# Six places for split pieces, gathering by two experts, folding by matmul, and fewer native down pieces in a mixture of experts

## The chip, the cores and the metric

The kernel runs on one core of a Trainium2 chip, as one program. Its time is the device time in microseconds (us); 1911.24 us is the median of three runs of the kernel before. TensorE (PE in the rows, its weight loads PEld) multiplies, VectorE (DVE) and ScalarE (ACT) work element by element, GpSimd (POOL) and SyncE (SP) here mostly issue DMA transfers.

## The reference

A small transformer in float32 for 256 tokens of width 1024: a first block (modulated norms, differential attention beside a Fourier mixer, and a hierarchical mixture of experts), and then a second block with four feed-forward layers and two mixers. The change lies in the mixture of experts:

```python
def hier_moe(h, w_rg, b_rg, w_re, b_re, w_gate, w_up, w_down):
    ...
    top_val, top_idx = lax.top_k(e_in, TOP_K)          # 2 of the 8 experts of one group
    gate = p_grp * jax.nn.softmax(top_val, axis=-1)
    expert = grp[:, None] * EXPERTS_PER_GROUP + top_idx
    ...
    def expert_block(args):
        tok, wt, e = args
        xb = h_pad[tok]
        y = (jax.nn.silu(xb @ w_gate[e]) * (xb @ w_up[e])) @ w_down[e]
        return y * wt[:, None]
```

There are 32 experts. `w_gate[e]` and `w_up[e]` are 1024 x 512, `w_down[e]` is 512 x 1024, so that 6.3 MB of weights are read for each expert.

## The kernel before

**Precision.** TensorE has a plain FP32 product and a shorter one of type FP32R. The kernel takes most of its products in FP32R, with each operand split in two: ScalarE casts a weight piece to FP32R (`wh`, line 152), VectorE subtracts the cast from the piece (`wl`, line 153), and TensorE multiplies with both (`split`, line 150). A "native" piece is not split; TensorE multiplies it from its raw buffer in plain FP32.

**The stream of weights.** All weights come in pieces of 128 x 2048 (1 MB), in one list, `stream`. `load` issues the next piece's DMA on SP's queue into one of five `raw` buffers, or during the experts into the one buffer of `rawx`. `run_loads` keeps at most so many loads ahead of the oldest piece that isn't finished. A split piece is finished when its split is emitted (its buffer comes free when VectorE has done `wl`), a native piece when its product is. `ahead(3)` emits splits until three pieces wait, into four pairs of `wh` and `wl` (pool `split`); `take` hands out the next.

**An expert.** Up to 64 tokens of an expert have slots. `hot` makes one-hot matrices `G` for four experts, `gather` multiplies the normed rows (high part `xh` and low part `xl`) with `G` into `XG`, whose 128 columns are the 64 high and the 64 low parts of an expert's tokens. `rows(e, which)` multiplies `XG` as the stationary operand with two pieces of the gate (`which` 0) or up weights (1), 32 matmuls of 512 columns for both, and copies the result to `gu` on ScalarE. Its rows 0 to 63 belong to the high, 64 to 127 to the low parts; `turn` transposes `gu`, sums the two halves, and makes silu(gate) times up, split into `act`. `down` multiplies `act` with the two pieces of the down weights and scales to `yh`, `yl`; `place` transposes `G`, and `scatter` adds `yh` and `yl` to the four banks `bank_acc` with it.

The second down piece of every expert is native (`NATIVE`, all four residues of `e % 4`). The loop over the experts is a pipeline:

```python
for e in range(34):
    if 0 < e < 33: turn(e - 1)
    if e < 32: rows(e, 0); ...; gather(...); rows(e, 1); place(e)
    if e > 1: scatter(e - 2)
    if 0 < e < 33: down(e - 1)
```

The framework puts the emitted instructions in order for each engine; on the chip each engine then takes its own in that fixed order, and a waiting instruction holds what stands behind it.

Of the kernel before, what the change touches and what calls it, by code (L numbers as in the profile page):

```python
# [10 lines left out]
F32 = mybir.dt.float32  # L11
F32R = mybir.dt.float32r
# [6 lines left out]
P = 128  # L19
# [2 lines left out]
EPS = 1e-6  # L22
PIECE = 2048
RAW = 5
NX = 1
NEG = -1e30
SEL = -3e38

# [1 line left out]
class Net:  # L30
    def __init__(self, ctx, tc, I, out):
        self.ctx, self.tc, self.nc, self.I, self.out = ctx, tc, tc.nc, I, out
        self.cp = self.pool(ctx, "const", 1)
        self.rawp = self.pool(ctx, "raw", RAW)
        self.psp = ctx.enter_context(tc.tile_pool(name="psum", bufs=4, space=PSUM))
        self.hp = self.pool(ctx, "resid", 1)
        self.h = [self.hp.tile([P, D], F32, name=f"h{t}") for t in range(T)]
        self.xp = self.pool(ctx, "xT", 1)
        self.sp = self.pool(ctx, "small", 2)
        self.wp = self.pool(ctx, "split", 4)  # L40
        self.stream = []
# [3 lines left out]
        self.extra, self.extended, self.spare, self.slots_raw = {}, set(), 0, RAW  # L45
        self.parts = 1

    def pool(self, ctx, name, bufs):
# [8 lines left out]
    def load(self):  # L57
        src, shape, split = self.stream[self.loaded]
        n = int(np.prod(shape))
        if self.spare and self.loaded < self.moe_end:  # L60
            self.spare -= 1
            self.extended.add(self.loaded)
            raw = self.rawx.tile([P, PIECE], F32, name="rawx")
        else:
            raw = self.rawp.tile([P, PIECE], F32, name="raw")
        dst = self.shaped(raw, shape)
        if len(shape) == 3 and shape[1] == 2 and shape[2] == 256:
            for i in range(2):
                self.nc.sync.dma_start(dst[:, :, i, :], src[:, :, i, :])
        else:  # L70
            self.nc.sync.dma_start(dst, src)
        self.pieces[self.loaded] = raw
        for dst, src in self.extra.get(self.loaded, ()):
            self.nc.sync.dma_start(dst(), src)
        self.loaded += 1
# [7 lines left out]
    def run_loads(self):  # L83
        while self.free in self.done:
            self.done.discard(self.free)
            self.free += 1
        while self.loaded < len(self.stream) and self.loaded < self.free + self.slots_raw:
            self.load()

    def extend(self, ctx, n):  # L90

        self.rawx = ctx.enter_context(self.tc.tile_pool(name="rawx", bufs=n, reuse_waits="tile", side="right"))
        self.spare, self.slots_raw = n, RAW + n
        self.run_loads()

    def finished(self, i):
        self.done.add(i)
        if i in self.extended:
            self.spare += 1
        self.run_loads()  # L100

    def find(self, i, split):
# [4 lines left out]
    def ahead(self, n):  # L107

        while len(self.cutq) < n:
            i = self.find(self.cut, True)  # L110
            if i >= min(self.loaded, self.limit):
                return
            raw, shape = self.pieces[i], self.stream[i][1]
            k = int(np.prod(shape))
            wh = self.wp.tile([P, PIECE], F32R, name="wh")
            wl = self.wp.tile([P, PIECE], F32R, name="wl")
# [715 lines left out]
    def first(self):  # L832
# [3 lines left out]
        with ExitStack() as ctx:  # L836
# [376 lines left out]
            self.extend(self.xctx, NX)  # L1213
# [7 lines left out]
    def route_consts(self):  # L1221
        nc, I, cp = self.nc, self.I, self.cp
        self.idr = cp.tile([P, P], F32R, name="idr")
        nc.vector.tensor_copy(self.idr, self.idf)
        self.slots = cp.tile([P, P], F32, name="slots")
        nc.gpsimd.iota(self.slots, pattern=[[0, 2], [1, 64]], base=0, channel_multiplier=0,
                       allow_small_or_imprecise_dtypes=True)
        self.tri = cp.tile([P, P], F32, name="tri")
        nc.gpsimd.memset(self.tri, 1.0)
        nc.gpsimd.affine_select(out=self.tri, in_=self.tri, pattern=[[1, P]], compare_op=OP.is_gt, fill=0.0,  # L1230
                                base=0, channel_multiplier=-1)
        self.wr = cp.tile([P, 8, 36], F32, name="wr")
        nc.gpsimd.dma_start(self.wr[:, :, :4], I["w_router_group"][0].rearrange("(j p) e -> p j e", j=8))
        nc.gpsimd.dma_start(self.wr[:, :, 4:], I["w_router_expert"][0].rearrange("(j p) e -> p j e", j=8))
# [171 lines left out]
                            nc.vector.tensor_add(self.h[t][:, o], self.h[t][:, o], a)  # L1406


    NATIVE = ((0, 5), (1, 5), (2, 5), (3, 5))

    def native(self, e, n):

# [17 lines left out]
    def moe(self):  # L1430
        nc, I = self.nc, self.I
        self.limit = self.moe_end
        with ExitStack() as ctx:
            mp = self.pool(ctx, "moe", 1)
            XG, G, GT, gu, act, ys, acc = {}, {}, {}, {}, {}, {}, {}

            def hot(g):
# [6 lines left out]
            def gather(g, part):  # L1444

                if part == 0:
                    XG[g] = mp.tile([P, 4, 8, P], F32R, name="XG", bufs=2)
                jp, lo = part // 2, part % 2
                src = self.h2l if lo else self.h2h
                ps = self.bank().rearrange("p (j n) -> p j n", j=2)  # L1450
                for j in range(2):
                    for t in range(T):
                        self.mm(ps[:, j, :], src[t][:, P * (2 * jp + j) : P * (2 * jp + j) + P], G[g][:, t, :, :64],
                                start=t == 0, stop=t == 1)
                copy = nc.vector.tensor_copy if g == 0 and lo else nc.scalar.copy
                dst = XG[g][:, :, 2 * jp : 2 * jp + 2, 64 * lo : 64 * lo + 64].rearrange("p e j s -> p j e s")
                copy(dst, ps.rearrange("p j (e s) -> p j e s", e=4))  # L1457

            def place(e):
                ps = self.bank().bitcast(F32R)  # L1460
# [18 lines left out]
                return self.take_raw() if self.native(e, n) else self.take()  # L1479

            def rows(e, which):
                x = XG[e // 4][:, e % 4]
                ps = self.bank()
                for q in range(2):
                    product(ps, x, None, piece(e, 2 * which + q), 4, 4 * q, 7)
                    self.ahead(3)
                sb = mp.tile([P, 512], F32, name=f"gu{which}", bufs=1)

                nc.scalar.copy(sb.rearrange("s (a p) -> s a p", a=4), ps.rearrange("s (p a) -> s a p", a=4))
                gu[e, which] = sb  # L1490

            def turn(e):
                z = []
                for which in range(2):
# [9 lines left out]
                self.split(A[:, :, :64], A[:, :, 64:], z[0])  # L1504
                act[e] = A

            def down(e):
# [27 lines left out]
            self.second_rows(gnr)  # L1535
            self.parts = 4
            hot(0)
            for part in range(8):
                gather(0, part)
            self.weights(mp)  # L1540
            for e in range(34):
                if e == 1:
                    self.parts = 1
                if 0 < e < 33:
                    turn(e - 1)
                if e < 32:
                    rows(e, 0)
                    if e % 4 == 0 and e < 28:
                        hot(e // 4 + 1)
                if e < 32:  # L1550
                    if e < 28:
                        for i in range(2):
                            gather(e // 4 + 1, 2 * (e % 4) + i)
                    rows(e, 1)
                    place(e)
                if e > 1:
                    scatter(e - 2)
                if 0 < e < 33:
                    down(e - 1)
# [105 lines left out]
```

## Time and profile before

| | before |
|---|---|
| median of 3 runs | 1911.24 us (1909.47 to 1917.49) |
| the profiled execution | 1913.98 us, its span 1912.2 us |
| busy in the span: PE, DVE, ACT | 1837.8, 1327.7, 1146.4 us |
| mean granted TensorE clock | 0.99 of full |
| read from memory | 447.9 MB, 235 GB/s over the span |

The profile is of one execution. An engine's busy time is the time in which it has an instruction under way; matmuls overlap, so the step from start to start tells what one costs in a row of them, and a mean duration tells how long one takes to run through. A wait row names who waited and for whom. "Idle" in brackets is what the engine stood just before an instruction.

### The profile page before, as it was taken

How to read it: one execution, taken by the hardware profiler on the slowest of the kernel's cores; microseconds unless marked ns; L12 is line 12 of the kernel's file. 1: busy time of each engine (PE TensorE's matmuls, PEld its weight loads, DVE VectorE, ACT ScalarE, POOL GpSimd, SP SyncE). 2: the span in 40 equal slices, each digit the busy share in tenths (PEclk: the TensorE clock that was granted, in tenths of full speed). 3: DMA queues.
4: the chain of work that ended last, by engine and by line, in shares of the span. 5: the costliest groups of instructions: out<-in, count | busy, mean ns of one | idle time of the engine just before them, and what ended most of it. 6: DMA issues, size and time to landing. Idle time of an engine off the chain costs nothing.

```text
span 1912.2 us, 23030 instructions
## 1 busy us (share of the span) xinstructions
PE 1837.8 (96%) x8352; PEld 1439.9 (75%) x8352; DVE 1327.7 (69%) x2116; ACT 1146.4 (60%) x1924; POOL 41.8 (2%) x74
## 2 busy tenths in 40 slices
PE   6899699999999999999999999999999999999998
PEld 3677577766667666678888888887888888887886
DVE  2887788888888888865558765556555776765554
ACT  3555587778777777754456654446444755555443
POOL 2000000000000000000000000000000010100000
PEclk9999899999999999999999999999999999999999
DMA  9784398999999999865555455554555556665551
GB/s 301 257 284 144 111 340 356 349 357 353 351 357 352 353 365 367 277 220 177 179 179 178 155 176 198 198 186 153 190 198 198 182 172 198 199 218 191 181 180 43
DMA packets 189495, 450.51 MB, mean 236 GB/s; under 512 B 10170, under 2 KB 119066, under 8 KB 164802
## 3 DMA queue, kind: packets, MB, share of 16 engines
q1 hardware_dynamic: 185284, 437.26, 64.5%
q0 software_dynamic: 3808, 11.25, 2.1%
q8 instruction: 66, 1.08, 0.2%
q10 hardware_dynamic: 288, 0.52, 0.1%
q14 instruction: 49, 0.40, 0.1%
HBM read 447.92 MB, written 1.07 MB: 235 GB/s over the span
## 4 chain that ended last, share of the span: by engine, by line
PE 71%; DVE 8%; ACT 5%; issue 3%; DMA 1%; DVEq 0%; ACTq 0%; SPq 0%
PE bank_w L144 50%; PE bank_acc L144 17%; DVE wl L153 6%; ACT wh L152 3%; DMA raw<-w_up 1%; PE bank_w L1497 1%; PE bank_w L299 1%; ACT XG L1457 0%; PE bank_w L230 0%; ACT xh L233 0%; PE bank_w L702 0%; ACT L175 0%; DVE G L1440 0%; DVE yl L1521 0%; PE bank_w L490 0%
## 5 line engine op out<-in xcount | busy, mean ns | idle before, releaser
L153 DVE TENSOR_TENSOR wl<-raw,wh 128x512 fp32r<-128x512 f32 (+3 forms) x977 | 862.9, 936 | 301.4 <-ACT wh L152 299.0
L152 ACT CAST wh<-raw 128x512 fp32r<-128x512 f32 (+3 forms) x977 | 746.0, 823 | 285.2 <-PE bank_w L144 207.2
L144 PE MATMUL bank_w<-wh,xh 128*128 128x512 f32 (+2 forms) x1056 | 406.4, 385 | 4.1 <-ACT xh L233 3.4
L144 PE MATMUL bank_w<-wh,xl 128*128 128x512 f32 (+2 forms) x1056 | 402.7, 382 | 1.0 <-DVE xl L234 1.0
L144 PE MATMUL bank_w<-wl,xh 128*128 128x512 f32 (+2 forms) x1056 | 402.1, 381 | 0.0
L144 PEld LDWEIGHTS bank_w<-wh,xh 128*128 128x128 f32 x1056 | 199.0, 188 | 42.5 <-ACT xh L233 6.3
L144 PEld LDWEIGHTS bank_w<-wh,xl 128*128 128x128 f32 x1056 | 198.9, 188 | 38.0 <-DVE xl L234 2.5
L144 PEld LDWEIGHTS bank_w<-wl,xh 128*128 128x128 f32 x1056 | 199.0, 188 | 35.0 <-issue 0.2
L144 PE MATMUL bank_w<-wl,XG 128*128 128x512 f32 x512 | 208.7, 408 | 13.6 <-DVE wl L153 11.2
L144 PE MATMUL bank_w<-wh,XG 128*128 128x512 f32 x512 | 211.0, 412 | 0.1
L144 PE MATMUL bank_acc<-wh,th 128*128 128x512 f32 x352 | 144.2, 410 | 0.0
L144 PEld LDWEIGHTS bank_w<-wl,XG 128*128 128x128 f32 x512 | 96.0, 188 | 56.4 <-DVE wl L153 37.6
L144 PE MATMUL bank_acc<-wh,tl 128*128 128x512 f32 x352 | 137.7, 391 | 0.0
L144 PE MATMUL bank_acc<-wl,th 128*128 128x512 f32 x352 | 137.6, 391 | 0.0
L292 ACT ACTIVATE silu<-bank_w,rs 128x256 f32<-128x256 f32 x88 | 41.9, 476 | 155.4 <-PE bank_w L144 155.4
L294 DVE SCALAR_TENSOR_TENSOR hid<-bank_w,rs,silu 128x256 f32<-128x256 f32 x88 | 42.6, 484 | 116.7 <-ACT silu L292 113.3
L144 PEld LDWEIGHTS bank_w<-wh,XG 128*128 128x128 f32 x512 | 96.4, 188 | 23.2 <-issue 5.3
L144 PE MATMUL bank_w<-rawx,act 128*128 128x512 f32 x240 | 107.8, 592 | 0.0
L144 PEld LDWEIGHTS bank_w<-rawx,act 128*128 128x128 f32 x240 | 45.4, 189 | 45.5 <-issue 43.1
L144 PEld LDWEIGHTS bank_acc<-wh,tl 128*128 128x128 f32 x352 | 66.1, 188 | 14.1
L144 PEld LDWEIGHTS bank_acc<-wl,th 128*128 128x128 f32 x352 | 66.4, 189 | 11.2
L144 PEld LDWEIGHTS bank_acc<-wh,th 128*128 128x128 f32 x352 | 66.2, 188 | 11.1
(407 smaller groups left out, 2195.3 us busy)
## 6 DMA issues: line engine op xcount, KB each, us to landing
raw<-ffn_w_in SPq DMA_DIRECT2D x176, 512.0 KB, 4.7
raw<-w_up SPq DMA_DIRECT2D x64, 1024.0 KB, 7.9
raw<-w_gate SPq DMA_DIRECT2D x62, 1024.0 KB, 7.5
raw<-ffn_w_out SPq DMA_DIRECT2D x44, 1024.0 KB, 5.7
raw<-w_down SPq DMA_DIRECT2D x34, 1024.0 KB, 7.8
rawx<-w_down SPq DMA_DIRECT2D x30, 1024.0 KB, 6.4
raw<-w_ada SPq DMA_DIRECT2D x24, 1024.0 KB, 6.5
raw<-a_w_in SPq DMA_DIRECT2D x12, 1024.0 KB, 4.9
```

The costliest lines, as they stand in the source:

```text
L144: self.nc.tensor.matmul(*a, **k)
L152: self.nc.scalar.copy(h, src)
L153: self.nc.vector.tensor_sub(l, src, h.bitcast(F32))
L292: nc.scalar.activation(s, ps[:, :256], AF.Silu, scale=self.rs[t])
L294: nc.vector.scalar_tensor_tensor(hid[c, t], ps[:, 256:], self.rs[t], s, op0=OP.mult, op1=OP.mult)
L299: nc.tensor.transpose(ps[:, r, :], hid[c, t][:, P * r : P * r + P], self.idf)
L1497: nc.tensor.transpose(ps[:, P * a : P * a + P], gu[e, which][:, P * a : P * a + P], self.idf)
```

## The change

Four edits, in the mixture of experts:

- The buffer `rawx` goes. A pool `splitx` with two more pairs, `whx` and `wlx`, comes for the time of the experts; of every six splits two go there. `ahead(3)` stays.
- `XG` holds two experts rather than four (two buffers, as before). A gather matmul has 128 columns rather than 256, there are 32 of them for two experts rather than for four, and a copy out of PSUM still has 512 columns.
- `turn` multiplies `gu` with a constant `fold` (two identities of 64 x 64 above each other), which transposes and sums in one; eight transposes, two sums on VectorE and their two tiles go.
- The second down piece is native in the odd experts only.

The space for the descriptors of GpSimd's DMAs is set to 4096 bytes of a partition.

```diff
-            raw = self.rawx.tile([P, PIECE], F32, name="rawx")
-        else:
-            raw = self.rawp.tile([P, PIECE], F32, name="raw")
+        raw = self.rawp.tile([P, PIECE], F32, name="raw")
...
-        while self.loaded < len(self.stream) and self.loaded < self.free + self.slots_raw:
+        while self.loaded < len(self.stream) and self.loaded < self.free + RAW:
             self.load()
...
+            pool, x = self.wp, ""
+            if self.wx and i < self.moe_end:
+                self.cuts += 1
+                if self.cuts % (4 + SX) < SX:
+                    pool, x = self.wx, "x"
+            wh = pool.tile([P, PIECE], F32R, name="wh" + x)
+            wl = pool.tile([P, PIECE], F32R, name="wl" + x)
...
+        self.fold = cp.tile([P, 64], F32, name="fold")
+        nc.vector.tensor_add(self.fold, self.idf[:, :64], self.idf[:, 64:])
...
-    NATIVE = ((0, 5), (1, 5), (2, 5), (3, 5))
+    NATIVE = ((1, 5), (3, 5))
...
-                ps = self.bank().rearrange("p (j n) -> p j n", j=2)
-                for j in range(2):
+                e0 = 2 * (g % 2)
+                ps = self.bank().rearrange("p (j n) -> p j n", j=4)
+                for j in range(4):
                     for t in range(T):
-                        self.mm(ps[:, j, :], src[t][:, P * (2 * jp + j) : P * (2 * jp + j) + P], G[g][:, t, :, :64],
-                                start=t == 0, stop=t == 1)
+                        self.mm(ps[:, j, :], src[t][:, P * (4 * jq + j) : P * (4 * jq + j) + P],
+                                G[g // 2][:, t, e0 : e0 + 2, :64], start=t == 0, stop=t == 1)
...
             def turn(e):
-                z = []
+
+                ps = self.bank().rearrange("p (w a s) -> p w a s", w=2, a=4)
                 for which in range(2):
-                    ps = self.bank()
                     for a in range(4):
-                        nc.tensor.transpose(ps[:, P * a : P * a + P], gu[e, which][:, P * a : P * a + P], self.idf)
-                    r = mp.tile([P, 4, 64], F32, name=f"sum{which}", bufs=1)
-                    nc.vector.tensor_reduce(r, ps.rearrange("p (a i s) -> p a s i", a=4, i=2), axis=AX.X, op=OP.add)
-                    z.append(r)
-                nc.scalar.activation(z[0], z[0], AF.Silu)
-                nc.vector.tensor_mul(z[0], z[0], z[1])
+                        self.mm(ps[:, which, a, :], gu[e, which][:, P * a : P * a + P], self.fold, start=True, stop=True)
+                z = mp.tile([P, 4, 64], F32, name="z", bufs=1)
+                nc.scalar.activation(z, ps[:, 0], AF.Silu)
+                nc.vector.tensor_mul(z, z, ps[:, 1])
...
-            for part in range(8):
+            for part in range(4):
                 gather(0, part)
...
-                    if e < 28:
+                    if e < 30:
                         for i in range(2):
-                            gather(e // 4 + 1, 2 * (e % 4) + i)
+                            gather(e // 2 + 1, 2 * (e % 2) + i)
...
-    nc = bacc.Bacc("TRN2", target_bir_lowering=False, num_devices=1)
+    nc = bacc.Bacc("TRN2", target_bir_lowering=False, num_devices=1, dynamic_dma_scratch_size=4096)
```

The edits also move instructions in the fixed orders. ScalarE's order before, from the up copy of expert 26 to the gate copy of expert 27 (`sum` is the silu, `act` the copy of its split, `wh` the casts of pieces):

```order
L1489 COPY gu_5549<-bank_w 128x512
L1501 ACTIVATE sum_5603<-sum_5603 128x256
L152 CAST act<-sum_5603 128x4x64
L152 CAST wh<-raw 128x2048
L1520 ACTIVATE yh<-bank_w,gslot 128x512 x2
L152 CAST wh<-raw 128x2048
L1457 CAST XG<-bank_w 128x2x4x64
L152 CAST wh<-raw 128x2048
L1457 CAST XG<-bank_w 128x2x4x64
L152 CAST wh<-raw 128x2048
L1489 COPY gu_5646<-bank_w 128x512
```

The same place of ScalarE's order after, between the same two copies (`z` is the silu; the down piece that ends ahead of `yh` is a native one, that of expert 25):

```order
L1488 COPY gu_5764<-bank_w 128x512
L1464 COPY GT<-bank_w 128x256
L148 CAST wh<-raw 128x2048
L1517 ACTIVATE yh<-bank_w,gslot 128x512 x2
L148 CAST wh<-raw 128x2048
L1498 ACTIVATE z<-bank_w 128x256
L148 CAST whx<-raw 128x2048
L1456 CAST XG<-bank_w 128x4x2x64
L148 CAST act<-z 128x4x64
L148 CAST whx<-raw 128x2048
L1488 COPY gu_5857<-bank_w 128x512
```

The first cast now stands ahead of the silu, and the silu and the copy of `act` have moved behind the second `yh`; four casts stand between the two copies in both orders.

Earlier in the stage the order after is another. ScalarE from the up copy of expert 10 to the first XG copy behind the gate copy of expert 11:

```order
L1488 COPY gu_3440<-bank_w 128x512
L148 CAST wh<-raw 128x2048
L1464 COPY GT<-bank_w 128x256
L148 CAST wh<-raw 128x2048
L1517 ACTIVATE yh<-bank_w,gslot 128x512 x2
L148 CAST wh<-raw 128x2048
L1498 ACTIVATE z<-bank_w 128x256
L148 CAST act<-z 128x4x64
L148 CAST wh<-raw 128x2048
L1488 COPY gu_3533<-bank_w 128x512
L1456 CAST XG<-bank_w 128x4x2x64
```

The first cast behind the up copy is here that of the next expert's first up piece; at expert 26 it is that of the next expert's first gate piece. Two pieces more are cast ahead of the up copy here.

On TensorE, at the down piece and the turn of expert 26, before:

```order
L144 MATMUL bank_w<-wh,act 128x512 x2
L1497 MATMUL bank_w<-idf,gu_5510 128x128 x4
L1497 MATMUL bank_w<-idf,gu_5549 128x128 x4
L144 MATMUL bank_w<-wl,act 128x512
L144 MATMUL bank_w<-wh,act 128x512
L144 MATMUL bank_w<-wl,act 128x512 x2
L144 MATMUL bank_w<-wh,act 128x512
L144 MATMUL bank_w<-wl,act 128x512
L144 MATMUL bank_w<-rawx,act 128x512 x4
L144 MATMUL bank_w<-wh,XG 128x512
```

And after:

```order
L140 MATMUL bank_w<-wh,act 128x512 x2
L140 MATMUL bank_w<-fold,gu_5716 128x64 x4
L140 MATMUL bank_w<-fold,gu_5764 128x64
L140 MATMUL bank_w<-wl,act 128x512
L140 MATMUL bank_w<-wh,act 128x512
L140 MATMUL bank_w<-wl,act 128x512 x2
L140 MATMUL bank_w<-wh,act 128x512
L140 MATMUL bank_w<-wl,act 128x512
L140 MATMUL bank_w<-raw,act 128x512 x4
L140 MATMUL bank_w<-fold,gu_5764 128x64 x3
```

Five of the eight products with `fold` stand ahead of the native piece and three behind it; before, all eight transposes stood ahead of it.

## Rows read from the trace of the kernel before

**Rows 1.** Busy by stretch: start:end, length, PE, PEld, DVE, ACT, POOL, clock, DMA, GB/s.

```profile
262.00:770.00 508.00, 494.09 (x2121) 354.55 (x2119) 431.31 (x331) 382.30 (x399) 0.59 (x1) 1.00 0.94 358
830.00:1912.20 1082.20, 1069.26 (x5005) 890.54 (x5003) 662.75 (x1348) 581.73 (x1217) 19.95 (x35) 1.00 0.54 179
```

**Rows 2.** The tile rawx: ns min/median/max, first and last start in us.

```profile
L71 SPq DMA_DIRECT2D rawx<-w_down x30: 327/328/328, 258.3 to 769.7; - x30
```

**Rows 3.** TensorE in time over one expert: start, length in us.

```profile
396.91 0.64 PE L144 MATMUL bank_w<-G,xh 128*128 128x256 f32 x4
...
397.39 1.09 PE L144 MATMUL bank_acc<-yh,GT 128*128 128x512 f32 x4
...
398.32 0.39 PE L144 MATMUL bank_w<-wl,XG 128*128 128x512 f32 x1
...
398.55 0.39 PE L144 MATMUL bank_w<-wh,XG 128*128 128x512 f32 x1
...
403.70 0.28 PE L1462 MATMUL bank_w<-idr,G 128*128 128x128 f32 x2
...
408.55 1.03 PE L1497 MATMUL bank_w<-idf,gu 128*128 128x128 f32 x8
...
410.80 3.59 PE L144 MATMUL bank_w<-rawx,act 128*128 128x512 f32 x8
```

**Rows 4.** Who waited for whom, 262 to 770 us: total, times, longest.

```profile
ACT gu L1489 <- PE bank_w L144: 52.3, 31, 3.0
...
PEld bank_w L144 <- DVE wl L153: 36.2, 69, 1.9
ACT sum L1501 <- DVE sum L1499: 29.5, 27, 2.4
```

**Rows 5.** Groups by shape, 262 to 770 us: busy us, mean ns, idle before.

```profile
L153 DVE TENSOR_TENSOR wl<-raw,wh 128x2048 fp32r<-128x2048 f32 x143 | 326.6, 2291 | 51.7 <-ACT wh L152 49.8
L152 ACT CAST wh<-raw 128x2048 fp32r<-128x2048 f32 x142 | 271.6, 1917 | 3.4 <-DMA raw<-w_gate 1.7 <-PE bank_w L144 1.4 <-DMA raw<-w_up 0.2
...
L144 PE MATMUL bank_w<-rawx,act 128*128 128x512 f32 x232 | 104.2, 592 | 0.0
...
L1499 DVE TENSOR_REDUCE sum<-bank_w 128x256 f32<-128x512 f32 x60 | 38.9, 686 | 10.4 <-PE bank_w L1497 10.4
...
L1457 ACT CAST XG<-bank_w 128x512 fp32r<-128x512 f32 x52 | 30.5, 592 | 0.4 <-PE bank_w L144 0.4
L1497 PE MATMUL bank_w<-idf,gu 128*128 128x128 f32 x232 | 30.1, 272 | 0.0
```

**Rows 6.** ScalarE in time from one up copy on.

```profile
408.28 0.59 ACT L1489 COPY gu<-bank_w 128x512 f32<-128x512 f32 x1 [1.75 <-PE bank_w L144]
...
409.91 0.42 ACT L1501 ACTIVATE sum<-sum 128x256 f32<-128x256 f32 x1 [1.04 <-DVE sum L1499]
...
411.03 0.40 ACT L152 CAST act<-sum 128x256 fp32r<-128x256 f32 x1 [0.71 <-DVE sum L1502]
...
411.34 1.89 ACT L152 CAST wh<-raw 128x2048 fp32r<-128x2048 f32 x1
...
414.43 0.69 ACT L1520 ACTIVATE yh<-bank_w,gslot 128x512 fp32r<-128x512 f32 x1 [0.60 <-PE bank_w L144]
```

**Rows 7.** Plain FP32 products of few columns: router's loads in time; attention's group.

```profile
206.66 0.97 PEld L144 LDWEIGHTS bank_w<-wr,xaT 128*128 128x128 f32 x8 [0.91 <-ACT xaT L1250]
...
L144 PE MATMUL bank_acc<-v,aT 128*128 128x128 f32 x64 | 8.4, 276 | 0.0
```

**Rows 8.** The chain that ended last, at the stage's start.

```profile
226.82 1.85 PE bank_w L144 x7
...
233.62 4.97 PE bank_w L144 x24
```

**Rows 9.** DMA issues: count, KB each, median us to landing.

```profile
raw<-w_gate SPq DMA_DIRECT2D x62, 1024.0 KB, 7.5
...
grp<-b_ln_b POOLq DMA_DIRECT2D x8, 192.0 KB, 6.3
```

More of the change, by code (lines that the diff above doesn't have):

```diff
@@ L24 @@
 RAW = 5
-NX = 1
+SX = 2
 NEG = -1e30
@@ L44, in __init__ @@
         self.pieces = {}
-        self.extra, self.extended, self.spare, self.slots_raw = {}, set(), 0, RAW
+        self.extra, self.wx, self.cuts = {}, None, 0
         self.parts = 1
@@ L59, in load @@
         n = int(np.prod(shape))
-        if self.spare and self.loaded < self.moe_end:
-            self.spare -= 1
-            self.extended.add(self.loaded)
-            raw = self.rawx.tile([P, PIECE], F32, name="rawx")
-        else:
-            raw = self.rawp.tile([P, PIECE], F32, name="raw")
+        raw = self.rawp.tile([P, PIECE], F32, name="raw")
         dst = self.shaped(raw, shape)
@@ L86, in run_loads, with extend @@
             self.free += 1
-        while self.loaded < len(self.stream) and self.loaded < self.free + self.slots_raw:
+        while self.loaded < len(self.stream) and self.loaded < self.free + RAW:
             self.load()
[L90 to L94, printed above, removed]
+    def extend(self, pool):
+        self.wx, self.cuts = pool, 0
     def finished(self, i):
         self.done.add(i)
-        if i in self.extended:
-            self.spare += 1
         self.run_loads()
@@ L114, in ahead @@
             k = int(np.prod(shape))
-            wh = self.wp.tile([P, PIECE], F32R, name="wh")
-            wl = self.wp.tile([P, PIECE], F32R, name="wl")
+            pool, x = self.wp, ""
[5 more added lines that the diff above has]
+            wl = pool.tile([P, PIECE], F32R, name="wl" + x)
             for o in range(0, k, k // self.parts):
@@ L1212, in first @@
             c2.close()
-            self.extend(self.xctx, NX)
             self.route_pre(1, ap, a2)
@@ L1434, in moe @@
             mp = self.pool(ctx, "moe", 1)
+            self.extend(self.pool(ctx, "splitx", SX))
             XG, G, GT, gu, act, ys, acc = {}, {}, {}, {}, {}, {}, {}
@@ L1446, in gather @@
                 if part == 0:
-                    XG[g] = mp.tile([P, 4, 8, P], F32R, name="XG", bufs=2)
-                jp, lo = part // 2, part % 2
+                    XG[g] = mp.tile([P, 2, 8, P], F32R, name="XG", bufs=2)
+                jq, lo = part // 2, part % 2
                 src = self.h2l if lo else self.h2h
-                ps = self.bank().rearrange("p (j n) -> p j n", j=2)
-                for j in range(2):
+                e0 = 2 * (g % 2)
+                ps = self.bank().rearrange("p (j n) -> p j n", j=4)
+                for j in range(4):
                     for t in range(T):
-                        self.mm(ps[:, j, :], src[t][:, P * (2 * jp + j) : P * (2 * jp + j) + P], G[g][:, t, :, :64],
-                                start=t == 0, stop=t == 1)
+                        self.mm(ps[:, j, :], src[t][:, P * (4 * jq + j) : P * (4 * jq + j) + P],
+                                G[g // 2][:, t, e0 : e0 + 2, :64], start=t == 0, stop=t == 1)
                 copy = nc.vector.tensor_copy if g == 0 and lo else nc.scalar.copy
-                dst = XG[g][:, :, 2 * jp : 2 * jp + 2, 64 * lo : 64 * lo + 64].rearrange("p e j s -> p j e s")
-                copy(dst, ps.rearrange("p j (e s) -> p j e s", e=4))
+                dst = XG[g][:, :, 4 * jq : 4 * jq + 4, 64 * lo : 64 * lo + 64].rearrange("p e j s -> p j e s")
+                copy(dst, ps.rearrange("p j (e s) -> p j e s", e=2))
             def place(e):
@@ L1481, in rows @@
             def rows(e, which):
-                x = XG[e // 4][:, e % 4]
+                x = XG[e // 2][:, e % 2]
                 ps = self.bank()
@@ L1492, in turn @@
             def turn(e):
-                z = []
+                ps = self.bank().rearrange("p (w a s) -> p w a s", w=2, a=4)
                 for which in range(2):
-                    ps = self.bank()
                     for a in range(4):
-                        nc.tensor.transpose(ps[:, P * a : P * a + P], gu[e, which][:, P * a : P * a + P], self.idf)
-                    r = mp.tile([P, 4, 64], F32, name=f"sum{which}", bufs=1)
-                    nc.vector.tensor_reduce(r, ps.rearrange("p (a i s) -> p a s i", a=4, i=2), axis=AX.X, op=OP.add)
-                    z.append(r)
-                nc.scalar.activation(z[0], z[0], AF.Silu)
-                nc.vector.tensor_mul(z[0], z[0], z[1])
+                        self.mm(ps[:, which, a, :], gu[e, which][:, P * a : P * a + P], self.fold, start=True, stop=True)
+                z = mp.tile([P, 4, 64], F32, name="z", bufs=1)
+                nc.scalar.activation(z, ps[:, 0], AF.Silu)
+                nc.vector.tensor_mul(z, z, ps[:, 1])
                 A = mp.tile([P, 4, P], F32R, name="act", bufs=2)
-                self.split(A[:, :, :64], A[:, :, 64:], z[0])
+                self.split(A[:, :, :64], A[:, :, 64:], z)
                 act[e] = A
```

## The prediction

> **What bounds the kernel now.** I read the busy time by stretch first. The mixture of experts fills 226 to 790 us, and its even part, 262 to 770 us, is where all four edits act. There TensorE is busy 494 of 508 us, VectorE 431, ScalarE 382, and the DMA engines are 0.94 busy at 358 GB/s; the 1082 us from 830 us on are TensorE at 99% with the DMA at 0.54, and no edit touches that code [rows 1]. So two resources are near full in the stage at once, and the reader should look for the slack of each.
>
> The period comes from the loads of the native down pieces, one an expert: 30 of them from 258.3 to 769.7 us, 511.4 / 29 = **17.63 us an expert** [rows 2].
>
> Busy TensorE counts the running out of each matmul, so I rebuilt its work from starts. A 512-column FP32R matmul follows the last one after 0.23 (398.32 to 398.55; four from 397.39 to 398.32 take 0.93), a 256-column gather matmul after 0.12 (four from 396.91 to 397.39) [rows 3]. Eight transposes take 1.03 with the last one's 0.27, so 0.109 each; eight native instructions 3.59 with the last one's 0.59, so 0.428 each [rows 3, 5]. A piece of 4 native products shows 8 records: a plain FP32 product is two instructions. An expert's work: rows 32 x 0.23 = 7.36, split down piece 8 x 0.23 = 1.84, native piece 8 x 0.428 = 3.42, scatter 8 x 0.23 = 1.84, gather 8 x 0.12 x 28/32 = 0.84, turn 8 x 0.109 = 0.87, place 0.28: **16.45**. The other 1.2 us of the period is TensorE standing.
>
> Why it stands: mostly for the second half of a split, wl from VectorE (36.2 us in the table of waits), while ScalarE itself loses 52.3 us at the gu copies and 29.5 at the sums [rows 4]. One expert shows the loop. The up copy starts at 408.28; the silu waits 1.04 for VectorE's sums, and the next cast starts only at 411.34, 3.06 later; the second yh starts at 414.43, when the native piece is done, and ends 6.84 after the copy [rows 6]. Three casts and two XG copies follow in ScalarE's order (3 x 1.92 + 2 x 0.59 = 6.94, less about 0.1 for each of five overlaps: 13.3), then wl (2.29) and the last eight matmuls (1.84): 17.4 [rows 5]. That is the period. Before is thus a **chain through ScalarE, VectorE and TensorE**, with one cast of reserve at each up copy.
>
> **The change part by part.**
> *Native pieces in every second expert.* 16 pieces go from 3.42 to 1.84: -1.58 x 16 = **-25.3 us** of TensorE. ScalarE and VectorE each split 16 pieces more (1.92 and 2.29 us): half of that an expert, +0.96 and +1.15 [rows 5].
> *Turn by matmul.* 8 one-record transposes become 8 plain FP32 products, 16 instructions, each with its own 128-column weights. No such product with 64 columns stands in the even part. The nearest row has 36 columns: eight loads back to back take 0.97 with 0.19 for the last, 0.111 each, however few columns follow [rows 7]. So 16 x 0.111 = 1.78 against 0.87: +0.91 x 32 = **+29 us** of TensorE. It frees VectorE of two sums of 0.686 an expert [rows 5], and takes a station out of the silu's chain.
> *Gather by two experts.* 256 matmuls of 256 columns become 512 of 128. FP32R products of 128 columns are not in the trace. Lower bound: the FP32R transposes in place, the second 0.06 after the first (0.28 less the 0.22 that one takes) [rows 3]; upper bound: a plain FP32 product of 128 columns, two records of 8.4 / 64 = 0.131, so 0.26 [rows 7]. I take 0.111, since weights of the same size must be loaded for each and the 36-column row shows that this alone sets the step. In the loop 480 x 0.111 = 53.3 against 224 x 0.12 = 26.9: **+26 us**. The copies stay two an expert.
> The Trainium skill, "TensorE: Matmul & The Clock Gate", section "Back-to-back issue gap", gives about 81 ns for a matmul of 128 columns and 131 ns for one of 512 in a stream of loads and matmuls. This trace's 512-column step is 0.23, so I do not follow it; by it the gather would cost 480 x 0.03, an estimated 14 us less.
> *Six places for split pieces.* They take nothing off any engine; they let casts run further ahead. The raw buffers fall from six to five, so that all places together go from ten to eleven. In ScalarE's printed order I counted casts against the pieces used up by each up copy: before, one cast of reserve from expert 5 on; after, two to six up to expert 17, and one or two from 18 on.
> *Start.* The first gather fills one XG of two experts: four copies rather than eight. Its matmuls run from 226.82 to 233.6, waiting on copies, and the first rows start at 233.62 [rows 8]. With half of the copies I take **-2.5 us** (0 to -3.4, half of it).
> *The smaller descriptor space and the fold constant* I cost at nothing: the POOL queue's loads are for the stages behind, where 1082 us of TensorE work cover them; without that cover one such load is 6.3 us late [rows 1, 9].
>
> TensorE after, per expert: 7.36 + 1.84 + 0.28 + (3 x 1.84 + 3.42) / 2 + 16 x 0.111 x 30/32 + 1.78 = **17.4**, 0.95 more than before and 0.23 under the present period. The change trades TensorE's standing for TensorE's work. ScalarE's busy 382 / 28.8 = 13.3 rises to 14.3, VectorE's 15.0 falls by 0.2 [rows 1]. The DMA needs 0.94 x 17.63 = 16.6 us an expert, still under 17.4.
>
> **The sum.** Experts 2 to 17 have reserve, so that the chain above is cut and TensorE paces them: 17.4 and about 0.1 for what is left of waits, -0.13 x 18 = -2.3 (with the first two).
> From 18 on the printed order again has one cast of reserve, and I follow the chain. With a native piece: the rest of the scatter 0.46, split down piece 1.84, five turn products 1.11, native 3.42, and 0.2 until ScalarE sees it: the second yh ends at 7.7 rather than 6.84. Then cast, silu, cast, XG, act, cast: 3 x 1.92 + 0.42 + 0.59 + 0.40 - 0.5 = 6.7, wl 2.29, eight matmuls 1.84: 18.5. Without one: copy and cast of the second down piece end at 2.45, its wl at 4.74, its matmuls at 6.1, the second yh at 7.0; three casts, XG and act 6.75 - 0.4, wl, matmuls: 17.5. Mean 18.0, +0.37 for about 12 experts: +4.5 [rows 5, 6].
> -2.3 + 4.5 - 2.5 = -0.3 us: **no change**. The profiled execution took 1913.98 (span 1912.2 and 1.8 around it), 2.7 above the median of 1911.24; taken from there the sum gives 1913.7, from the median 1911. I say 1912. This kernel's measurement tells about 0.5%, 9.6 us, from no change.
>
> **The rivals.**
> A, slower: the supply binds in all experts. A native piece now holds one of only five raw buffers until TensorE has used it, and loads are issued in stream order, so the fifth load behind it cannot be issued before. Five pieces of 17.63 / 6 us are the whole cover of a landing of 7.5 and a split of 4.2 [rows 9, 5]. For it: the DMA has 0.94 x 17.63 = 16.6 of 17.4 to do. Against: three pieces behind the native one are already split by then. It decides once a hole of more than 1.6 us (twice 17.4 - 16.6) opens per native piece. Then each expert takes 18.0 to 18.4: +11 to +23 us less the start, 1920 to 1932.
> B, slower: a 128-column FP32R product costs like plain FP32: 480 x 0.15 = +72, 1984. Only the bound of rows 7 speaks for it.
> C, faster: the loads of FP32R weights step at 0.06 as in place: 480 x 0.05 = 24 us less TensorE; the DMA's 16.6 becomes the bound at 16.8, so about 20 less: 1892. The 36-column row speaks against it, though it is plain FP32. The skill's 81 ns, as cited, would be part of this.
> D, no change or just faster: the late order does not bind, because the earlier reserve is never used up on the chip. TensorE paces all 30: -0.23 x 30 - 2.5 = -9.4, 1902.
>
> **How the numbers follow.** Forecast 0.55 (1903 to 1921), A 0.20, B 0.04, C 0.06, D 0.15. Faster by over 0.5% is under 1901.7: C, a good third of D and a little of the forecast's lower end, 0.13. Slower is over 1920.8: B, most of A and the forecast's upper end, 0.30. The rest, 0.57, is no change. 1900 to 1930 leaves out C, B, and the ends of A and D: two in ten.
>
> **What would show it.** In the changed kernel's even part: fold matmuls in steps of 0.11, 128-column gather matmuls in steps of 0.11 (0.06 is C, 0.22 and more is B); loads of a second-expert native piece 35 us apart in the first half and 36 in the second; the waits of TensorE for wl near nothing up to expert 17 and back after it; ScalarE's sum waits gone. If the native loads are 36 or more apart from the start, with the DMA share under 0.9 and ScalarE waiting for raw, it is A. The prediction is wrong above all if the reserve counted in the printed order is not what paces the chip, or if the small matmuls are not held by their weight loads.

## The result, and the profile after

The changed kernel took **1925.24 us** (median of 5 runs, 1924.58 to 1928.19), the kernel before 1911.33 on the same chip: a ratio of 1.0071, 95% interval [1.0052, 1.009]. It is slower by 0.7%, and beyond the 1920.8 from which the prediction called it slower. The profiled execution of after took 1927.08 us with a span of 1925.3, 13.1 more than the span of before.

First the busy time of the kernel after by stretch, with the columns of [rows 1]: the even part of the experts, the stages behind it, and two stretches of 100 us inside the even part.

```profile
262.00:770.00 508.00, 500.75 (x2552) 403.73 (x2550) 412.44 (x282) 403.64 (x409) 0.58 (x1) 1.00 0.93 347
830.00:1925.30 1095.30, 1082.44 (x5048) 900.55 (x5046) 665.86 (x1354) 582.18 (x1219) 19.96 (x35) 1.00 0.54 179
...
300.00:400.00 100.00, 100.00 (x519) 81.58 (x518) 82.44 (x55) 82.41 (x84) 0.00 (x0) 1.00 0.93 352
600.00:700.00 100.00, 96.82 (x490) 77.41 (x490) 79.20 (x52) 78.58 (x80) 0.00 (x0) 1.00 0.93 340
```

TensorE never stands in the first stretch of 100 us and does 519 matmuls there; in the second it stands 3% and does 490. VectorE, ScalarE and the loads slow down with it, from 352 to 340 GB/s. So the stage has two regimes. Where one ends shows in the place step, two transposes an expert: its rows in both kernels, each over three stretches. The last numbers are its first and last start, so eight, ten and thirteen experts lie between them. Before:

```profile
L1462 PE MATMUL bank_w<-idr,G x18: 220/224/227, 243.0 to 368.5; 128*128 128x128 f32 x18
L1462 PE MATMUL bank_w<-idr,G x22: 221/223/227, 368.5 to 546.5; 128*128 128x128 f32 x22
L1462 PE MATMUL bank_w<-idr,G x28: 220/223/230, 546.4 to 776.5; 128*128 128x128 f32 x28
```

And after:

```profile
L1461 PE MATMUL bank_w<-idr,G x18: 221/224/229, 244.0 to 374.8; 128*128 128x128 f32 x18
L1461 PE MATMUL bank_w<-idr,G x22: 221/225/229, 374.8 to 549.0; 128*128 128x128 f32 x22
L1461 PE MATMUL bank_w<-idr,G x28: 220/224/232, 549.0 to 786.2; 128*128 128x128 f32 x28
```

The 13.1 us fall apart like this (in rounded parts, 13.0). The first place is 1.0 later. Experts 0 to 8 take 130.8 instead of 125.5: +5.3. Experts 8 to 18 take 174.2 instead of 178.0, **17.42 an expert** instead of 17.80: -3.8. Experts 18 to 31 take 237.2 instead of 230.1, 18.25 instead of 17.70: +7.1. From the last place to the end it is 1139.1 instead of 1135.7: +3.4. The kernel after wins only in the middle. The 18.25 is a mean: from its 25th place to its 29th (657.5 and 732.4 us) an expert takes 18.7.

The steps of the small matmuls stand in TensorE's timeline of after (start, length):

```profile
404.15 1.00 PE L140 MATMUL bank_w<-G,xh 128*128 128x128 f32 x8
404.99 1.06 PE L140 MATMUL bank_w<-G,xl 128*128 128x128 f32 x8
405.89 0.45 PE L140 MATMUL bank_w<-wh,XG 128*128 128x512 f32 x1
...
413.48 3.59 PE L140 MATMUL bank_w<-raw,act 128*128 128x512 f32 x8
416.91 1.89 PE L140 MATMUL bank_w<-fold,gu 128*128 128x64 f32 x16
418.61 0.48 PE L140 MATMUL bank_w<-whx,XG 128*128 128x512 f32 x1
```

Sixteen gather matmuls of 128 columns take 405.89 - 404.15 = 1.74, so 0.109 each; sixteen turn instructions of 64 columns (eight products) take 1.70, 0.106 each; eight native ones 3.43, 0.429 each, as in [rows 3].

The waits of after that answer to [rows 4], 262 to 770 us (total, times, longest):

```profile
DVE wl L149 <- ACT wh L148: 53.5, 54, 2.4
ACT yh L1517 <- PE bank_w L140: 41.4, 37, 2.6
ACT gu L1488 <- PE bank_w L140: 38.1, 28, 3.0
...
PEld bank_w L140 <- DVE wl L149: 8.1, 11, 1.6
...
ACT wh L148 <- DMA raw<-w_down: 2.4, 3, 1.3
```

The waits of TensorE's weight loads for wl fall from 36.2 to 8.1 (2.2 more are for `wlx`), and all of these lie behind 550 us; the sum waits of ScalarE are gone. The casts wait little for loads from memory (2.4 for down pieces, 3.1 in all). In the late stretch the chain that ended last (start, length, what) reads:

```profile
634.55 4.86 PE bank_w L140 x24
...
647.35 0.02 issue
647.37 1.38 ACT yh L1517 x2
648.75 1.80 ACT whx L148
650.56 0.02 issue
650.58 2.30 DVE wlx L149
652.88 0.04 issue
652.93 4.74 PE bank_w L140 x23
```

The path leaves TensorE for the two scaled outputs (`yh`), then one cast and one subtraction, 5.5 us in all, and comes back to it with the next piece. So the cast that TensorE needs next stands in ScalarE's order just behind a copy that waits for TensorE.

### The profile page after: what moved, and what is told of

Same layout as the page of the kernel before. It is cut to its first block, busy times and chain, and to the rows that moved or that the text cites. A ratio compares the mean times of both kernels' runs of the same rounds, so it can differ in the third digit from the quotient of the medians.

```text
span 1925.3 us, 24032 instructions
## 1 busy us (share of the span) xinstructions
PE 1857.9 (96%) x8864; PEld 1501.4 (78%) x8864; DVE 1316.4 (68%) x2067; ACT 1176.7 (61%) x1942; POOL 41.8 (2%) x74
## 4 chain that ended last, share of the span: by engine, by line
PE 80%; DVE 3%; ACT 3%; issue 1%; ACTq 0%; DVEq 0%
PE bank_w L140 59%; PE bank_acc L140 19%; DVE wl L149 2%; ACT wh L148 1%; PE bank_w L295 1%; DVE wlx L149 1%; ACT whx L148 0%; ACT yh L1517 0%; PE bank_w L226 0%; ACT xh L229 0%; PE bank_w L698 0%; DVE xl L230 0%; ACT L171 0%; PE bank_w L1461 0%; PE bank_w L486 0%
## 5 line engine op out<-in xcount | busy, mean ns | idle before, releaser
L149 DVE TENSOR_TENSOR wl<-raw,wh 128x512 fp32r<-128x512 f32 (+3 forms) x930 | 768.4, 881 | 304.6 <-ACT wh L148 303.4
L148 ACT CAST wh<-raw 128x512 fp32r<-128x512 f32 (+3 forms) x930 | 666.3, 778 | 289.1 <-PE bank_w L140 207.5
L149 DVE TENSOR_TENSOR wlx<-raw,whx 128x2048 fp32r<-128x2048 f32 (+1 forms) x68 | 135.8, 2006 | 30.2 <-ACT whx L148 30.1
L140 PE MATMUL bank_w<-wl,XG 128*128 128x512 f32 x340 | 134.8, 396 | 5.4 <-DVE wl L149 5.2
L140 PE MATMUL bank_w<-wh,XG 128*128 128x512 f32 x340 | 136.4, 401 | 0.0
L148 ACT CAST whx<-raw 128x2048 fp32r<-128x2048 f32 (+1 forms) x68 | 113.4, 1683 | 5.2 <-PE bank_w L140 4.2
L140 PEld LDWEIGHTS bank_w<-wl,XG 128*128 128x128 f32 x340 | 63.9, 188 | 21.1 <-DVE wl L149 8.4
L140 PE MATMUL bank_acc<-wh,xh 128*128 128x512 f32 x160 | 67.7, 423 | 6.3 <-ACT xh L148 5.3
```

The lines of the kernel that those rows point to most:

```text
L140: self.nc.tensor.matmul(*a, **k)
L148: self.nc.scalar.copy(h, src)
L149: self.nc.vector.tensor_sub(l, src, h.bitcast(F32))
```

## The experiments

Each ratio is to the kernel before, measured beside it on the same chip. "In reserve" are pieces whose cast stands ahead of a copy in ScalarE's order and whose rows that copy does not need.

**Theory R, first form: the casts in reserve at each gu copy set the pace.** Four kernels. The first and the second put each gu copy of the kernel after, and of before, behind the last cast asked for:

```diff
-                nc.scalar.copy(sb.rearrange(...), ps.rearrange(...))
+                with self.tc.issue_after(self.lastcast.ins):
+                    nc.scalar.copy(sb.rearrange(...), ps.rearrange(...))
```

> The kernel after, with one thing changed: each gu copy is put behind the last cast emitted ahead of it in ScalarE's order, so that at least three pieces are cast beyond the rows it waits for; no work is added or taken away. Theory R (the reserve in ScalarE's order paces the late experts): from expert 18 on the pair falls from about 37.4 to 34.8 us, 11 us less, about 1914. Rival S (supply: five raw buffers and the DMA pace them): the casts then wait for raw and the time stays at 1925 or grows.

Measured: 1925.13 us, ratio 1.005 [1.0031, 1.0069], as slow as after. That is S's number, but not its reason: the casts wait 2.1 us for loads between 262 and 770 us. The printed order kept three casts in reserve at the up copies to the end, but the slow experts stayed (233.5 us from 18 to 31, after 237.2). ScalarE's waits of this run, 600 to 770 us, say where the wait went:

```profile
ACT yh L1519 <- PE bank_w L141: 19.2, 13, 2.6
ACT GT L1465 <- PE bank_acc L141: 11.8, 9, 2.4
```

In after the same stretch has 17.6 for yh, 14.3 for gu and 1.6 for GT. The gu waits are gone; yh waits a little more, and GT (the copy of the transposed `G`) has taken their place. The expectation looked at one of three kinds of copy that wait for TensorE.

> The kernel before with the same one change of order. Theory R: the experts from 6 on fall from 17.5 (18.8 with a new G) to TensorE's 16.45 or the DMA's 16.6, 25 to 30 us less, about 1883. Rival S: the DMA and six raw buffers already pace them, no change, 1911.

Measured: 1933.78 us, 1.0097 [1.0079, 1.0116], slower than either theory said. In the kernel before the turn follows the up copy closely, and TensorE now waits for gu at the transposes (600 to 770 us):

```profile
PEld bank_w L1499 <- ACT gu L1491: 10.3, 9, 1.3
```

**The kernel after with the turn of before** (eight transposes and two sums instead of eight fold products of two instructions each):

```diff
-                        self.mm(ps[:, which, a, :], gu[e, which][:, P * a : P * a + P], self.fold, start=True, stop=True)
+                        nc.tensor.transpose(ps[:, P * a : P * a + P], gu[e, which][:, P * a : P * a + P], self.idf)
+                    nc.vector.tensor_reduce(r, ps.rearrange("p (a i s) -> p a s i", a=4, i=2), axis=AX.X, op=OP.add)
```

> The kernel after with the turn of before (eight transposes, two sums on VectorE). Theory R with TensorE's work as counted: 0.9 us less an expert, and the printed order keeps five to six casts of reserve to the end; 16.5 an expert, about 1895 (1900 if VectorE's 16.7 binds). Rival: VectorE or the supply binds and the matmul turn was worth its price: 1925 or more.

Measured: 1922.98 us, 1.0044 [1.0032, 1.0056]: a miss, although the printed reserve stayed at five or six. TensorE has less to do, but waits for VectorE's second half of the outputs (`yl`), and ScalarE for the sums (300 to 770 us):

```profile
ACT sum L1498 <- DVE sum L1496: 50.8, 26, 3.5
...
PEld bank_w L140 <- DVE yl L1518: 35.4, 25, 1.8
PE bank_w L140 <- DVE yl L1518: 24.4, 23, 1.3
```

The casts also wait 21.9 us for loads in this stretch, far more than in after; which of these waits sets this run's pace stays open. So a reserve of casts alone does not make TensorE the pace, and the turn by matmul by itself did not make the change slow.

**The kernel after with four places** (SX = 0):

> The kernel after with four places for split pieces rather than six. Theory R: the reserve in the printed order falls to one or two at expert 12 rather than 18, six experts more run at 18.7 rather than 17.4: 8 us more, about 1933. Rival: the places bind nowhere, 1925.

Measured: 1937.62 us, 1.0118 [1.01, 1.0137]. The first eight experts are as in after, but the slow experts begin in the next ten (180.5 us instead of 174.2):

```profile
L1460 PE MATMUL bank_w<-idr,G x18: 221/224/229, 244.0 to 374.5; 128*128 128x128 f32 x18
L1460 PE MATMUL bank_w<-idr,G x22: 221/225/229, 374.5 to 555.0; 128*128 128x128 f32 x22
```

Here R was right in the place, and some 5 us low in the time: the stock sets where the slow stretch begins. What sets its pace was still open; the loads (the prediction's rival A) were the next suspect.

**Theory L: the loads.** More load buffers, by the mechanism that the kernel before had (NX extra ones; the second run has SX = 0 and NX = 2):

```diff
-SX = 2
+SX = 1
+NX = 1
...
+            self.extend_raw(self.xctx, NX)
```

> The kernel after with one extra load buffer from the start of the experts (six in all, as before the change) and five places for split pieces instead of six. Theory L (the loads are the supply: with five load buffers they bring 340 GB/s in the slow stretch, so the 12.6 MB of a pair of experts take 37 us): at the 357 GB/s that six buffers brought in the kernel before, a pair takes 35.2 us or less, the seven slow pairs lose some 13 us, and the time is 1912 (1905 to 1918). Theory R (the stock of split pieces, worn down by the place of the casts in ScalarE's order, is what ends): one place fewer begins the slow stretch earlier, as with four places, and the time is 1931 (1925 to 1938).

Measured: 1925.81 us, 1.0065 [1.0045, 1.0084]. L missed. It lies at the edge of R's range, but R's reason failed: with one place fewer the slow stretch did not begin earlier (experts 0 to 18 in 305.1 us, after 305.0).

> The kernel after with two extra load buffers (seven in all) and four places for split pieces. It differs from the run with four places and five load buffers (1937.6) in the load buffers alone. Theory L: the loads come at 360 GB/s or more, TensorE's 34.8 us a pair is reached nearly everywhere, and the time is 1912 (1904 to 1920). Theory R: as with four places before, 1937 (1931 to 1943).

Measured: 1924.91 us, 1.0054 [1.0033, 1.0074]. Neither number. The place rows of this run:

```profile
L1476 PE MATMUL bank_w<-idr,G x38: 221/225/229, 247.0 to 551.7; 128*128 128x128 f32 x38
L1476 PE MATMUL bank_w<-idr,G x28: 220/224/230, 551.7 to 788.3; 128*128 128x128 f32 x28
```

Experts 0 to 18 take 304.7 us and 18 to 31 take 236.6; after took 305.0 and 237.2. Five loads and six places, six and five, seven and four: eleven in all, and the same course. The stock counts both kinds alike. The late pace does not move with two more load buffers, and from 600 to 770 us no cast of this run waits for a load. That speaks against the loads as its cause; the run with five load buffers and the mended order, below, rules them out.

> The kernel before with a seventh load buffer (the room for it comes from a smaller descriptor area for the software queue, as the change has it too). Theory L: its experts took 17.5 us from the eighth on at 357 GB/s, against 16.4 to 16.6 us of TensorE; a seventh buffer lifts the loads to 365 GB/s or more, 0.4 to 0.9 us an expert over some 24 experts, and the time is 1898 (1888 to 1906). Theory R: the stock of split pieces in its four places is used up as before, 1911 (1907 to 1914).

Measured: 1913.76 us, 0.9998 [0.9988, 1.0007]. Here R hit, and L missed: a seventh buffer in the kernel before changes nothing.

**An unsplit piece in every expert again** (NATIVE as before, all else as after):

> The kernel after with one unsplit down piece in every expert again (as before the change), so with less work for ScalarE, VectorE and TensorE, and still five load buffers. Theory L: an unsplit piece keeps its load buffer until its matmuls, now in every expert, so the loads come at less than 340 GB/s, an expert takes 18.5 to 19 us after the first few, and the time is 1938 (1928 to 1955). Theory R: the stock of six places is never used up, TensorE's some 16.7 us an expert sets the pace, and the time is 1905 (1895 to 1912).

Measured: 1932.51 us, 1.01 [1.0081, 1.0119]. It lies in L's range, but L's reason did not hold, and R's premise of 16.7 us was my slip: by the prediction's own terms an expert of after with a native piece costs TensorE 17.4 + 1.58 / 2 = 18.2. TensorE is 100% busy from 300 to 700 us, and the row of the place step gives (763.2 - 270.9) / 27 = **18.23 us an expert**:

```profile
L1461 PE MATMUL bank_w<-idr,G x56: 221/225/229, 270.9 to 763.2; 128*128 128x128 f32 x56
```

This is the purest run of the study for TensorE's terms: the small matmuls of turn and gather, added to the work of before, are the pace and TensorE waits for nothing, although ScalarE's casts wait 36.8 us for loads between 262 and 770 us. Halving the native pieces is worth 18.2 against 17.4 where order permits.

**Theory C: the length of the way through one cast and one subtraction.** Pieces cast and subtracted in two halves (self.parts = 2 instead of 1 from expert 1 on), in both kernels:

> The kernel after with each weight piece of the experts cast and subtracted in two halves of 1024 columns instead of one of 2048, so that TensorE can begin with the first half. Theory C (in the slow stretch the way from TensorE's output through ScalarE's copy, then the cast of the next piece, 1.9 us, then its subtraction, 2.3 us, back to TensorE is what the pair waits for; the loads landed some 4 us before and are not waited for): the way gets up to 2 us shorter once an expert, the seven slow pairs fall from 37.1 to 34.8 us, and the time is 1912 (1907 to 1918). Theory S (ScalarE and VectorE can do no more pieces in the time): more instructions, so 1930 or more (1927 to 1940).

Measured: 1924.25 us, 1.005 [1.0035, 1.0065]: neither number. In its profile experts 18 to 31 took 232.9 us instead of 237.2, but the time did not follow; the profiled execution is the slowest of this kernel (1928.55), with its first place at 249.8 us, 5.7 later than in after.

> The kernel before with each weight piece of the experts cast and subtracted in two halves. Theory C: its experts took 17.5 us (18.8 every fourth) from the eighth on, against 16.4 of TensorE, by the same way through one cast and one subtraction; they come to 16.4 to 16.8 us, 24 experts by 0.8 us, and the time is 1892 (1885 to 1902). Theory S: 1920 or more.

Measured: 1931.68 us, 1.009 [1.0071, 1.011]: S's side, but not its reason either, since ScalarE was 0.74 to 0.78 and VectorE 0.80 to 0.84 busy between 300 and 700 us. The largest wait is now VectorE's for yh (600 to 770 us); that the halves brought it about by moving other instructions in the queues is not shown by a run of its own:

```profile
DVE yl L1521 <- ACT yh L1520: 27.8, 9, 3.1
PEld bank_w L144 <- DVE wl L153: 23.4, 54, 1.3
...
ACT yh L1520 <- PE bank_w L144: 16.7, 9, 1.9
```

**Theory O: the order alone.** The kernel after with gu and yh both behind the last cast asked for, and five pieces asked for ahead instead of three:

```diff
-                    self.ahead(3)
+                    self.ahead(5)
...
-                    nc.scalar.activation(yh, ps[half], AF.Copy, scale=gs)
+                    with self.tc.issue_after(self.lastcast.ins):
+                        nc.scalar.activation(yh, ps[half], AF.Copy, scale=gs)
```

> The kernel after with both the copies of the rows (gu) and the scaled outputs (yh) on ScalarE issued behind the last cast that was asked for, and five pieces asked for ahead instead of three, so that ScalarE's order keeps five pieces in stock at every such copy. Theory O (the place of the casts behind the copies that wait for TensorE is all that makes the late pairs 37.1 us): they stay at 34.8, and the time is 1912 (1908 to 1917). Theory S (ScalarE and VectorE, or the loads, can not deliver 11 pieces in 34.8 us, whatever the order): as with the gu copies alone, 1925 (1921 to 1935).

Measured: **1909.57 us, 0.9977 [0.9967, 0.9987]**. O hit. Its work, places and load buffers are those of after. Busy time and place rows:

```profile
300.00:400.00 100.00, 100.00 (x515) 81.52 (x515) 82.53 (x54) 81.98 (x84) 0.00 (x0) 1.00 0.94 357
600.00:700.00 100.00, 100.00 (x513) 81.25 (x512) 83.08 (x57) 81.60 (x84) 0.00 (x0) 1.00 0.91 359
```

```profile
L1462 PE MATMUL bank_w<-idr,G x22: 221/225/229, 373.7 to 549.2; 128*128 128x128 f32 x22
L1462 PE MATMUL bank_w<-idr,G x28: 221/225/229, 549.1 to 773.6; 128*128 128x128 f32 x28
```

TensorE is 100% busy in the late stretch too, with 513 matmuls against 490. Experts 8 to 18 take 17.55 us each, and 18 to 31, with the shorter last ones, 224.5 against after's 237.2. From 600 to 770 us no gu copy waits for TensorE and the yh copies wait 0.9 us in all. Here is the up copy of expert 25, with a cast right ahead of it and no wait:

```profile
673.59 1.91 ACT L149 CAST whx<-raw 128x2048 fp32r<-128x2048 f32 x1
675.40 0.59 ACT L1490 COPY gu<-bank_w 128x512 f32<-128x512 f32 x1
675.87 1.92 ACT L149 CAST wh<-raw 128x2048 fp32r<-128x2048 f32 x1
```

In after the same copy stood behind a wait of 1.92 us, and the next cast behind it:

```profile
679.03 0.59 ACT L1488 COPY gu<-bank_w 128x512 f32<-128x512 f32 x1 [1.92 <-PE bank_w L140]
679.51 1.90 ACT L148 CAST wh<-raw 128x2048 fp32r<-128x2048 f32 x1
```

The run does not part its two edits (yh too, and five ahead). Nor does it mend every copy: those of XG, z and GT still wait 24.5 us for TensorE in 600 to 770 us, and TensorE, with five pieces in stock, does not stand. The late experts are 12.8 us of the gain in this profile; another 8.2 lie behind the last place (1131.0 against 1139.1 us), which the theory doesn't speak of.

**The same order with the gather of before** (by four experts, five places, four pieces ahead):

> The order of the last run (gu and yh behind the last cast asked for) with the gather by four experts of the kernel before in place of the gather by two, and five places with four pieces asked for ahead, since the wider gather takes the room of the sixth. Theory T (with the order mended TensorE alone sets the pace, so its instructions are the price): 16 instructions of 128 columns fewer an expert at 0.111 us, against 8 wider ones, is some 0.8 us an expert over 30 experts, 34.8 us a pair becomes 33.2, and the time is 1886 (1880 to 1892). Theory D (the loads are next: at 33.2 us a pair they would have to bring 379 GB/s, and no stretch of 100 us here showed over 371): pairs of 34 to 35 us, and the time is 1901 (1893 to 1910).

Measured: 1920.18 us, 1.0031 [1.002, 1.0042]: both missed. TensorE stands 5.8% of 600 to 700 us, although four pieces stay in reserve at the up copies. The chain runs from ScalarE's z through a cast and its subtraction to yl on VectorE, and TensorE waits for yl (600 to 770 us):

```profile
ACT z L1499 <- PE bank_w L141: 23.5, 9, 2.7
...
PEld bank_w L141 <- DVE yl L1520: 7.6, 8, 1.5
...
PE bank_w L141 <- DVE yl L1520: 4.5, 6, 1.1
```

Here z has become the copy with a cast behind it, and on VectorE yl stands behind a subtraction of 2.3 us. What the gather by two costs in time with a good order stays open.

## Why the prediction was right and where it was not

The forecast was 1912 in a range of 1900 to 1930. The time is in the range, on the slower side that had 0.30. But it lies outside the 1903 to 1921 of the forecast's own mechanism and inside the 1920 to 1932 of rival A, whose mechanism the runs rule out. So the range held in part by luck: it was wide enough for a sum of -0.3 us that came out as +13.1. What held is TensorE's work and the cause of the late stretch; the other terms have to be read one by one.

*TensorE's work, right.* The prediction counted 17.4 us an expert; 8 to 18 measured 17.42, and with a native piece everywhere 18.23 against its 18.2. The step of 0.111 for a small matmul measured 0.109 (gather) and 0.106 (turn); rivals B and C, which hung on it, are out. The Trainium skill, "TensorE: Matmul & The Clock Gate", section "Back-to-back issue gap", has some 81 ns for 128 columns; the row's 0.109 decides against following it here.

*Experts 2 to 17: the step that failed.* "Period 17.63 an expert" was a mean over 30 loads that I took as uniform. Before had two regimes as well: with its own reserve of three casts up to expert 3, it went from its second place (253.4 us) to its ninth (368.5) in 16.44 us an expert, TensorE's own 16.45, and only then at 17.80:

```profile
L1462 PE MATMUL bank_w<-idr,G x16: 220/224/227, 253.4 to 368.5; 128*128 128x128 f32 x16
```

So the added TensorE work was paid in full in the first eight (+5.3) and gained back in the next ten (-3.8): +1.5 over 0 to 18, in place of -2.3. The prediction named that reserve and used it for after alone.

*From 18 on: right in place and cause, mis-sized.* It put the change of regime at expert 18 by the printed order, and there it is. It took 18.0 an expert against 17.63, +4.5 for 12; measured 18.25 against 17.70, +7.1 for 13, with 18.7 in the steady experts. The chain is the one named: output, cast, subtraction, TensorE. That order makes it is shown by the run with gu and yh behind the casts and five pieces ahead, which changes nothing of the work and takes it away.

*Rival A, out.* Six and seven load buffers leave the late pace at 236.6 to 237.2 us for 13 experts, and 8 to 18 ran at TensorE's 17.42 with five. Rival D, that the earlier reserve is never used up, is out in the kernel as it stands; the mended order gives what D spoke of, TensorE's pace to the end.

*Start, wrong.* -2.5 came from half the copies. The first gather has 32 matmuls in both kernels, and in after all of them ran at the lower clock (first the busy row of a stretch, then TensorE in time):

```profile
226.00:235.00 9.00, 9.00 (x39) 8.61 (x39) 8.26 (x19) 5.39 (x11) 0.00 (x0) 0.50 0.35 117
...
225.58 0.44 PE L140 MATMUL bank_w<-G,xh 128*128 128x128 f32 x1 [5.81 <-DVE G L1438]
...
232.44 0.58 PE L140 MATMUL bank_w<-r_W,r_hot 128*128 128x32 f32 x2
232.83 0.77 PE L140 MATMUL bank_w<-whx,XG 128*128 128x512 f32 x1
```

The granted clock is 0.50 there, the 1.2 GHz level (TensorE had been busy 2.3 of the 14 us before, from 212 to 226), and the matmuls step at 0.21, as those of 256 columns do at that level in before (starts 227.17, 227.38 and 227.59; the same stretch had 0.65 there). The gather takes 232.44 - 225.58 = 6.86 us against 233.62 - 226.82 = 6.80, so half the copies gave nothing. (At 233.62 stands a router matmul; the rows of before begin at 233.86, those of after 1.0 us earlier.) From the rows to the first place it is 11.2 us against 9.2, with part of the rows at the lower clock and a dearer gather in between. When the gather begins differs from profile to profile (223.6 to 230.9 us in the kernels with the new one), but from there to the first place all of these take 18.4 to 19.6 us, and the five with the old gather 15.5 to 16.3. So the term is about +2, not -2.5; the first place comes only 1.0 later because after's gather began 1.2 earlier in this profile.

*Behind the experts: +3.4 that nothing forecast.* The code is the same. Over the kernels of this study the way from the last place to the end was 1131.0 to 1141.8 us, so 3.4 lies within what one profile tells. Nor do the stretches at the lower clock tell the two apart by their length: behind the last place each profile has two of 3.4 us at 0.50. It is not explained.

## What to carry to other kernels

Before a mean period is used, cut the stage into stretches: a kernel that lives off a stock at first and off a chain later has two periods, and an edit that adds work to the engine at the bound is paid in the first. When two in-order engines wait for each other, look at every copy that waits and at what stands behind it. In the kernel after more buffers only put off the slow stretch, shorter pieces moved the wait, and an edit of the order took it away: two kinds of copy behind the casts, and a stock of five pieces. For the gu copies alone the same edit moved the wait to other copies, and in the kernel before it made things worse.

## What the runs showed that was not expected

Load buffers and places for split pieces were worth the same, one for one: 5 + 6, 6 + 5 and 7 + 4 gave 305.0, 305.1 and 304.7 us for experts 0 to 18. And ScalarE and VectorE need not be near full to hold TensorE up: in the late stretch of after each was 79% busy, the loads came at 340 GB/s against 359 with the better order, and TensorE still stood 3% of the time.
